# Sums of quarters stored unsplit, steps tied to their groups, and two gate tiles written in source order, in a one-core hybrid trunk kernel

## The chip, the cores and the metric

The kernel runs on one core of a Trainium2 chip. The metric is the device time of one execution in microseconds (us), from runs in which kernels take turns on the same chip. The engines named below are TensorE (PE, with its weight loads PEld), VectorE (DVE), ScalarE (ACT), GpSimd (POOL) and SyncE (SP). SP and POOL issue nearly all DMAs here, each in the order of its own instruction queue.

## The reference, cut to what matters

The program is one layer of a decoder trunk, on 512 prompt tokens and 8 single-token samples, which stand side by side as 520 columns.

```python
def mixer(xn, ...):
    proj = xn @ w_in                       # 2048 x 6160
    bg, cg, hin, q, k, v, og, glr = jnp.split(proj, ...)
    cu, conv_new = causal_dwconv(cg * hin, conv_prev, conv_w)
    ya = bg * cu
    o, s_new = gla_chunked(qh, kh, vh, lf, gla_prev, chunk)
    yb = rms(o) * gla_norm_g * silu(og)
    return concatenate([ya, yb]) @ w_out   # 2048 x 2048

def conv_ffn(xn, prev, w_up, conv_w, conv_b, w_down):
    u, v = jnp.split(xn @ w_up, 2)         # 2048 x 11264
    cu, new = causal_dwconv(u, prev, conv_w)
    return (silu(cu + conv_b) * v) @ w_down, new   # 5632 x 2048

x = x + mixer(rmsnorm(x, norm_mix_g))
x = x + conv_ffn(rmsnorm(x, norm_ffn_g))
y = rmsnorm(x, final_norm_g)
```

## The kernel before

**Numbers.** Every float32 operand of a large product is used as two parts: `hi`, a rounded copy made by ACT, and `lo`, the rest, made by DVE as operand minus `hi` (`split`, L115; `parts`, L101; `prepare`, L1163). A product is three matmuls: hi by hi, hi by the lo of x, lo of the weight by hi. Activations lie transposed, 128 features by 520 columns, as a `hi` and a `lo` tile.

**Stages.** First x is transposed to `xT_d` in DRAM and to the split tiles `xa`. Then come the *plain* groups (`group`, L165): 128 output columns, 16 steps of the contraction, 96 matmuls of 260 columns. For each of the four GLA heads h these are k, q and two of v, and behind each head a tile of the short convolution (`conv_tile`, three groups: cg, hin, bg). The GLA recurrence of a head is a generator in `queue`, of which `tick` takes a step four times a group. At the end of the plain stage stand two tiles of the output gate `og` (L1067). All else of `w_in`, and `w_out`, `w_up` and most of `w_down`, is done with seven products for eight: matrices are seen as 2 by 2 blocks, and `ORDER` lists the seven products, 24 matmuls each. Their weights are raw blocks or sums of blocks, made by DVE (`s<-raw`, L1123) from four loads of 512 KB (`weights`, L1110), and then split. Their activations are seven *forms* of x: forms 1 to 3 are quarters of x themselves, and forms 4 to 7 are sums of quarters. `MIX` lists nine groups of w_in, then follow 8 groups of w_out ("wo"), 44 of w_up ("up") and 20 of w_down ("down").

**Where the sums come from.** For w_in, `mixer_sums(g)` (L665) loads four quarters of x for each g of 0 to 3 from `xT_d`, scales them with the norm's weight on ACT, makes t1, t2, t4 and t3 on DVE and hands each to `stored` (L625): ACT copies hi, DVE subtracts lo, and two DMAs of 260 KB on POOL put them into `mt_d`. That makes 16 sums and 32 stores. `load_mixer_sums(g)` brings back hi and lo of each, 32 loads on POOL. For w_up, `projected(g)` (L1484) does the like behind each of the last four groups of w_out: it stores the new residual (`x1_d`), scales, makes the sums, and `out` (L1510) splits. Form 7, and all forms of the last g, go straight to their place; forms 5, 4 and 6 of g = 0 to 2 go as hi and lo through `t_d`, 18 stores and 18 loads on SP, since their places still hold the inputs of w_out. `load_sum` (L1554) loads them in the last group of w_out.

**What sets the order.** The framework orders the instructions of each engine by its own plan, from priorities (source order) and modelled costs. Where `InOrder` (L57) is called, source order is kept for the engines it names, by dependencies without semaphores. The start of the kernel and the loop over products from L1583 on are kept so; in the loop SP and POOL are kept too. The plain groups, the mixer sums and the two gate tiles are in the planner's order. `extra` (L171) holds the four generators of `mixer_sums`; `group` takes one step of it at its end, from head 1 on, which fixes its place in the source but not in the plan.

**The loop.** For product i, `prepare(i + 2)` splits the weights of two products ahead; `hi` and `lo` have three buffers. `run_steps` calls generators in `steps`, each of which yields the distance from its start, in products, of its next part. Raw weights of the current kind have three buffers (`raw` of pool `weights`), second halves four (pool `raw2`). The SBUF of the GLA pool is used again, after the plain stage, by the pools `yt2`, `raw2` and `sums`; that of `b12` by `yt3`. `yt1`, in place from early on, holds 4 of the 16 places of forms.

Of the kernel before, what the change touches and what calls it, by code (L numbers as in the profile page):

```python
# [37 lines left out]
def trunk_kernel(  # L38
# [18 lines left out]
    class InOrder:  # L57
# [9 lines left out]
        def all(self):  # L67
            return nc.cur_bb.bb.instructions

        def __call__(self):  # L70
# [18 lines left out]
    def two(ap):  # L89
        return ap.rearrange("p (a b) -> p a b", a=2)  # L90
# [565 lines left out]
    def first_tile(kind, g, m):  # L656

        return 4 * g + 2 * m if kind == "down" else 2 * g + 8 * m
# [5 lines left out]

    def mixer_sums(g):  # L665

        def place(n):
            return yt1.tile([P, T], F32, tag=f"y{'hl'[n % 2]}{n // 2 * 4}", name="yx")  # L670

        xg = [place(n) for n in range(4)]
        for q, x in enumerate(xg):
            nc.gpsimd.dma_start(two(x), rows_of(xT_d, "mix", g, q))
        yield
        for q, x in enumerate(xg):
            m = first_tile("mix", g, q // 2)
            for j, h in enumerate(halves(x)):
                nc.scalar.activation(h, h, AF.Copy, scale=gmix[:, m + j : m + j + 1])

        def out(f, t, hi):
            stored(t, [mt_d[f - 4, g, x] for x in range(2)], hi)

        yield
        t1, t2 = xg[0], place(4)
        sub(t1, xg[0], xg[1])
        minus(t2, t1, xg[3])
        out(5, t1, place(5))
        yield
        minus(xg[2], t2, xg[2])  # L690
        out(4, t2, place(6))
        out(7, xg[2], place(7))
        yield
        sub(xg[1], xg[3], xg[1])
        out(6, xg[1], place(5))

    def load_mixer_sums(g):
        for f in (5, 4, 7, 6):
            for x, t in enumerate(form(f, g)):
                nc.gpsimd.dma_start(t.bitcast(F32), mt_d[f - 4, g, x])  # L700

# [31 lines left out]
    with ExitStack() as mix:  # L733
        slots[0::4] = [yt1] * 4
        even, evp = {}, [None]

        def mixed(k):

            if k % 2:
                return tmp()[:, :T]  # L740
            if k < KD // 2:
                even[k] = evp[0].tile([P, T], F32, tag="ye", name="ye")
            else:
                even[k] = zpad[0][:, 2 : 2 + T]
            return even[k]

        def mixed_done(k, y):
            if k % 2 == 0:
                return
            he, dst, i = even.pop(k - 1), g_d[1 - k // 8], k // 2 % 4  # L750
            t21, t34 = pair_sums(he, y)
            for src, f in ((halves(he)[0], 6), (t21, 0), (t34, 2), (y, 4)):
                n = 1 if f == 6 else 2
                stored(src, [dst[f : f + n, x, i] for x in range(2)], tmp())


        def conv_tile(j):
# [10 lines left out]
            ps = group(w_in, j * P, xa)  # L768
            bgr, ya = tmp(), mixed(j)
            evac(ps, bgr[:, :T])  # L770
# [3 lines left out]
        with ExitStack() as gl:  # L774
# [255 lines left out]
            for h in range(NH):  # L1030
                if h == 1:
                    extra.extend(mixer_sums(g) for g in range(4))
                ps = group(w_in, 3584 + h * P, xa) if h else first[0]
# [22 lines left out]
            assert not queue and not extra, (len(queue), len(extra))  # L1056

        yctx = ctx.enter_context(ExitStack())
        yt2 = yctx.enter_context(tc.tile_pool(name="yt2", bufs=1, side="right"))
        slots[1::4] = slots[2::4] = [yt2] * 4  # L1060
        wxr = yctx.enter_context(tc.tile_pool(name="raw2", bufs=4, side="right"))
        wxp = yctx.enter_context(tc.tile_pool(name="sums", bufs=2, side="right"))
        early = second_half(lambda m, k: mix_source(0, m, k))
        for g in range(3):
            load_mixer_sums(g)

        for j in range(2):  # L1067
            og, e, on = tmp(), mixed(8 + j), tmp()
            nc.sync.dma_start(on[:, :T], o_d[j])
            ps = group(w_in, 5120 + j * P, xa)  # L1070
            evac(ps, og[:, :T])
            nc.scalar.activation(e, og[:, :T], AF.Silu)
            nc.vector.tensor_tensor(e, e, on[:, :T], op=ALU.mult)
            mixed_done(8 + j, e)

    bctx.close()
    slots[3::4] = [yctx.enter_context(tc.tile_pool(name="yt3", bufs=1))] * 4
    load_mixer_sums(3)
    for k in range(8):
        for f, kk, b in ((1, k, 0), (2, k + 8, 0), (3, k + 8, 1)):  # L1080
            xq[f, k] = [xa[kk][x][b] for x in range(2)]

# [205 lines left out]
    def mix_gate(n):  # L1288
# [24 lines left out]
        if what == "og":  # L1313
# [10 lines left out]
            mult(v, v, on[1])  # L1324
            yield 4
        dst, i = g_d[1 - k // 8], k // 2 % 4
        t21, t34 = pair_sums(u, v)

        late = n == len(MIX) - 1
        yield 9.5 if late else 4.5  # L1330
# [150 lines left out]

    ssq = []

    def projected(g):  # L1484
# [25 lines left out]
        def out(f, t):  # L1510

            if f == 7 or g == NG - 1:
                split(t, *form(f, g))
            else:
                hi = tmp()[:, :T]
                split(t, hi.bitcast(F32R), t.bitcast(F32R))
                for d, x in zip((t_d[f - 4, g, 0], t_d[f - 4, g, 1]), (hi, t)):
                    nc.sync.dma_start(d, x)

# [33 lines left out]

    def load_sum(f, g):  # L1554
        for x, d in zip(form(f, g), (t_d[f - 4, g, 0], t_d[f - 4, g, 1])):
            nc.sync.dma_start(x.bitcast(F32), d)

# [31 lines left out]
    steps, seeded = [], {}  # L1589
    finish = {"mix": mix_finish, "wo": chunk_finish, "up": up_finish, "down": chunk_finish}  # L1590
    for i, (kind, at, r) in enumerate(order):
# [17 lines left out]
        if j == 0:  # L1609
# [25 lines left out]
        if kind == "wo":  # L1635
# [172 lines left out]
```

## Time and profile before

| what | value |
|---|---|
| time, median of 3 runs | 2238.04 us (2236.33 to 2240.15) |
| the profiled execution's own time | 2237.56 us |
| its span | 2235.9 us, granted TensorE clock 0.987 |
| DVE busy / ACT busy / POOL busy | 78% / 50% / 22% of the span |
| DMA bytes | 430.42 MB, mean 193 GB/s |

The span is the profiled execution from its first to its last instruction; 1.7 us lie around it. A row of the page's groups gives the line, the engine, out<-in, the count, the busy time, the mean of one in ns and the idle time of the engine before them. In a timeline a bracket at the end of a row gives the idle time before it and what ended it. In the view of windows each stretch has its length, the busy time of each engine with the count of instructions, the granted clock, the busy share of the DMA engines (1.0 and a little over is full) and the rate in GB/s.

### The profile page before, as it was taken

What the parts mean: (1) busy time and instruction counts of PE and PEld (TensorE: products, weight loads), DVE (VectorE), ACT (ScalarE), POOL (GpSimd) and SP (SyncE); (2) the same over time, 40 slices, a digit from 0 to 9 for tenths busy, and PEclk for the clock granted to TensorE, in tenths of its full rate; (3) what the DMA queues carried; (4) which work ended last, traced back from release to release, by engine and by line L of the source; (5) the groups of instructions that cost most, each with busy time, mean ns of one, the idle gap of its engine ahead of it and who ended that gap; (6) DMA issues with size and microseconds to landing.
All of it is one profiled execution on the core that took longest, in us unless ns stands there. A gap on an engine that the chain in (4) does not pass through costs nothing.

```text
span 2235.9 us, 43902 instructions
## 1 busy us (share of the span) xinstructions
PE 2167.9 (97%) x17751; PEld 2141.5 (96%) x17751; DVE 1733.5 (78%) x2286; ACT 1114.3 (50%) x1629; POOL 487.5 (22%) x689
## 2 busy tenths in 40 slices
PE   8899999989999998999999999999999999999997
PEld 7889999989999998999999999999999999999997
DVE  5474473638887897888889989899898868888876
ACT  5454353424554475655555555555555554444445
POOL 3353141341223511111311222113121311010000
PEclk9999999999999999999999999999999999999999
DMA  8574444467788999576666766767667868784734
GB/s 249 188 225 123 118 139 120 123 191 211 186 234 262 288 272 300 142 187 172 181 182 165 194 167 182 183 162 194 176 176 198 283 187 224 241 249 142 228 105 152
DMA packets 470103, 430.42 MB, mean 193 GB/s; under 512 B 22489, under 2 KB 423285, under 8 KB 469757
## 3 DMA queue, kind: packets, MB, share of 16 engines
q1 hardware_dynamic: 422001, 289.58, 45.1%
q0 software_dynamic: 46576, 135.82, 22.7%
q8 instruction: 139, 2.28, 0.4%
q10 hardware_dynamic: 1324, 2.23, 0.3%
q14 instruction: 63, 0.52, 0.1%
HBM read 306.91 MB, written 87.76 MB: 177 GB/s over the span
## 4 chain that ended last, share of the span: by engine, by line
PE 83%; DMA 6%; DVE 4%; issue 2%; ACT 2%; SPq 1%; POOL 1%; ACTq 0%; DVEq 0%; POOLq 0%
PE mm L1202 33%; PE ms L1202 14%; PE mm L134 11%; PE x L1442 8%; PE y L1442 8%; PE e L1442 3%; PE f L1442 3%; DMA raw<-in_w_out_dram 1%; DMA yx<-xT_d 1%; PE ms L921 1%; DMA yl<-t_d 1%; DMA raw<-raw 1%; DMA t<-o_d 1%; DVE lo L106 1%; DVE lo L1182 1%
## 5 line engine op out<-in xcount | busy, mean ns | idle before, releaser
L1202 PE MATMUL mm<-yl,hi 128*128 128x260 f32 x1696 | 478.5, 282 | 3.6 <-DVE yl L118 2.8
L1202 PE MATMUL mm<-yh,hi 128*128 128x260 f32 x1696 | 480.0, 283 | 0.8 <-DMA yh<-t_d 0.7
L1202 PE MATMUL mm<-yh,lo 128*128 128x260 f32 x1696 | 478.8, 282 | 0.9 <-DVE lo L1182 0.9
L1178 ACT ACTIVATE hi<-raw 128x1024 fp32r<-128x1024 f32 x324 | 342.4, 1057 | 230.6 <-PE mm L1202 68.5
L1182 DVE TENSOR_TENSOR lo<-raw,hi 128x1024 fp32r<-128x1024 f32 x324 | 395.3, 1220 | 38.1 <-ACT hi L1178 37.6
L1182 DVE TENSOR_TENSOR lo<-s,hi 128x1024 fp32r<-128x1024 f32 x243 | 298.3, 1228 | 129.5 <-ACT hi L1178 124.3
L1178 ACT ACTIVATE hi<-s 128x1024 fp32r<-128x1024 f32 x243 | 257.1, 1058 | 217.0 <-DVE s L1123 79.5
L1202 PEld LDWEIGHTS mm<-yl,hi 128*128 128x128 f32 x1696 | 319.7, 188 | 4.4 <-DVE yl L118 3.0
L1202 PEld LDWEIGHTS mm<-yh,lo 128*128 128x128 f32 x1696 | 319.7, 188 | 1.2 <-DVE lo L1182 1.2
L1202 PEld LDWEIGHTS mm<-yh,hi 128*128 128x128 f32 x1696 | 319.1, 188 | 1.4 <-DMA yh<-t_d 0.7
L1202 PE MATMUL ms<-b,hi 128*128 128x260 f32 x1408 | 258.0, 283 | 0.0
L1202 PEld LDWEIGHTS ms<-b,hi 128*128 128x128 f32 x1408 | 218.1, 189 | 0.0
L1442 PE MATMUL x<-form,hi 128*128 128x260 f32 x1120 | 204.8, 283 | 4.3 <-DVE acc L1461 2.2
L1442 PE MATMUL y<-form,hi 128*128 128x260 f32 x1120 | 204.6, 283 | 2.7 <-DVE acc L1461 2.7
L1123 DVE TENSOR_TENSOR s<-s,raw 128x1024 f32<-128x1024 f32 x162 | 197.9, 1222 | 2.8
L1202 PE MATMUL ms<-b,lo 128*128 128x260 f32 x704 | 199.0, 283 | 0.0
L1442 PEld LDWEIGHTS x<-form,hi 128*128 128x128 f32 x1120 | 172.5, 188 | 5.2 <-issue 2.8
L1442 PEld LDWEIGHTS y<-form,hi 128*128 128x128 f32 x1120 | 172.5, 188 | 3.1 <-ACT hi L1178 3.0
L106 DVE TENSOR_TENSOR lo<-raw,hi 128x1024 fp32r<-128x1024 f32 x76 | 97.2, 1279 | 81.9 <-ACT hi L105 74.4
L1442 PE MATMUL y<-form,lo 128*128 128x260 f32 x560 | 158.4, 283 | 0.0
L1442 PE MATMUL x<-form,lo 128*128 128x260 f32 x560 | 158.3, 283 | 0.0
L1202 PE MATMUL mm<-bh,hi 128*128 128x260 f32 x424 | 121.7, 287 | 15.4 <-DVE t L492 12.6
(359 smaller groups left out, 5164.8 us busy)
## 6 DMA issues: line engine op xcount, KB each, us to landing
raw<-in_w_up_dram SPq DMA_DIRECT2D x176, 512.0 KB
raw<-in_w_down_dram SPq DMA_DIRECT2D x96, 512.0 KB
raw<-in_w_in_dram SPq DMA_DIRECT2D x92, 512.0 KB
form<-f_d SPq DMA_DIRECT2D x126, 260.0 KB
raw<-raw POOLq DMA_DIRECT2D x56, 512.0 KB, 5.9
f_d<-t POOLq DMA_DIRECT2D x80, 260.0 KB, 5.5
raw<-in_w_out_dram SPq DMA_DIRECT2D x32, 512.0 KB
form<-g_d POOLq DMA_DIRECT2D x42, 260.0 KB, 7.6
```

The costliest lines, as they stand in the source:

```text
L106: nc.vector.tensor_tensor(lo, raw, hi.bitcast(F32), op=ALU.subtract)
L134: nc.tensor.matmul(o, w, xx, start=first and i == 0, stop=last and i == 2)
L921: nc.tensor.matmul(pb[:, c * 64 : (c + 1) * 64], L[:, c, :], rhs[:, c], start=True, stop=True,)
L1123: return lambda: nc.vector.tensor_tensor(out, x, y, op=ALU.add)
L1178: nc.scalar.activation(his[i], src, AF.Copy)
L1182: nc.vector.tensor_tensor(los[i], src, his[i].bitcast(F32), op=ALU.subtract)
L1202: nc.tensor.matmul(st["bank"][b], w[:, k, :], x, start=b not in st["used"] and k == 0 and j == 0, stop=k == 7 and j == 2, skip_group_check ...
L1442: nc.tensor.matmul(ps[:, m, :], w[:, k, m * P : (m + 1) * P], x, start=b not in st["used"] and k == 0 and j == 0, stop=k == 3 and j == 2, ...
```

## The change

`mt_d` and `t_d` lose their dimension of hi and lo: a sum goes to DRAM as one float32 tile, and is split after it comes back. `mixer_sums` becomes one generator over g = 1, 2, 3, 0, whose loads are on SP; three of the sums of g = 0 stay in SBUF and are split there, so 13 sums are stored. `group` ties each step of it behind the last instruction that the source has so far on each engine. The two gate tiles move behind the creation of `in_order`, are written out with their loads ahead, and so stand in source order, with the loads of the sums (on SP now), their splits and the start of the first products between them. The second gate's activation and the sums of the two gate tiles (`leave`, formerly the end of `mix_gate`) become steps of the first products. For w_up, nine splits (`split_sums`) follow nine loads at fixed steps of the last group of w_out. `MIX` and the loop are as before.

```diff
+        def after_all(self):
+            self.last = {i.engine: i.name for i in self.all()}
+            return self
...
-        if extra and next(extra[0], extra) is extra:
-            extra.popleft()
+        if extra:
+            step = InOrder(nc.gpsimd.engine, nc.sync.engine).after_all()
+            if next(extra[0], extra) is extra:
+                extra.popleft()
+            step()
...
-    t_d = dp.tile([3, 4, 2, P, T], F32, name="t_d")
-    mt_d = dp.tile([4, 4, 2, P, T], F32, name="mt_d")
+    t_d = dp.tile([3, 3, P, T], F32, name="t_d")
+    mt_d = dp.tile([4, 4, P, T], F32, name="mt_d")
...
+    def mixer_sums():
+        def place(n):
+            return yt1.tile([P, T], F32, tag=f"y{n}", name="yx")
+        for g in (1, 2, 3, 0):
+            xg = [place(n) for n in ("l0 h8 l8 h0" if g % 2 else "l1 l4 h4 h0").split()]
+            for q, x in enumerate(xg):
+                nc.sync.dma_start(two(x), rows_of(xT_d, "mix", g, q))
+            yield
+            for q, x in enumerate(xg):
+                m = first_tile("mix", g, q // 2)
+                for j, h in enumerate(halves(x)):
+                    nc.scalar.activation(h, h, AF.Copy, scale=gmix[:, m + j : m + j + 1])
+                if q == 1:
+                    yield
+            yield
+            t1, t3, t4, b22 = xg
+            t2 = place("h1")
+            sub(t1, t1, t3)
+            minus(t2, t1, b22)
+            yield
+            if g:
+                for f, t in ((5, t1), (4, t2)):
+                    nc.gpsimd.dma_start(mt_d[f - 4, g], t)
+            sub(t3, b22, t3)
+            minus(t4, t2, t4)
+            yield
+            nc.gpsimd.dma_start(mt_d[3, g], t4)
+            if g:
+                nc.gpsimd.dma_start(mt_d[2, g], t3)
+        for f, t in ((5, t1), (6, t3), (4, t2)):
+            split(t, *form(f, 0))
...
+                nc.sync.dma_start(t_d[f - 4, g], t)
...
+    def load_sum(d, f, g):
+        hi, lo = form(f, g)
+        x = lo.bitcast(F32)
+        nc.sync.dma_start(x, d[f - 4, g])
+        return lambda: split(x, hi, lo)
+
+    def split_sums():
+        for n in (4, 4.5, 5.5, 6, 6.5, 7.5, 8.5, 9, 9.5):
+            yield n
+            loaded.popleft()()
...
     in_order = InOrder(nc.gpsimd.engine, nc.sync.engine)
-    mult(R2, R, R)
...
+    raws = [load_og(n) for n in range(3)]
+    ws = [parts(*raws[0])]
+    raws.append(load_og(3))
+    early = second_half(lambda m, k: mix_source(0, m, k))
+    on = [tmp()[:, :T] for _ in range(2)]
+    for j, x in enumerate(on):
+        nc.sync.dma_start(x, o_d[j])
+    put = [load_sum(mt_d, f, g) for f in (5, 4) for g in range(1, 4)]
+    ws.append(parts(*raws[1]))
+    ps = new_mm()
+    span(ps, ws[0], xa, 0, 0, 8, KD)
+    ws.append(parts(*raws[2]))
+    span(ps, ws[1], xa, 8, 8, 8, KD)
+    ws.append(parts(*raws[3]))
     begin(0)
     load_rest(0)
+    put += [load_sum(mt_d, 6, g) for g in range(1, 4)]
+    y8, y9 = zpad[0][:, 2 : 2 + T], tmp()[:, :T]
+    evac(ps, y8)
+    nc.scalar.activation(y8, y8, AF.Silu)
+    mult(y8, y8, on[0])
+    ps = new_mm()
+    span(ps, ws[2], xa, 0, 0, 8, KD)
     prepare(0)
+    for x in put[:3]:
+        x()
+    span(ps, ws[3], xa, 8, 8, 8, KD)
     prepare(1)
+    for x in put[3:6]:
+        x()
+    evac(ps, y9)
+    mult(R2, R, R)
...
+    put += [load_sum(mt_d, 7, g) for g in range(4)]
...
+    def second_gate():
+        yield 0.5
+        nc.scalar.activation(y9, y9, AF.Silu)
+        yield 1
+        mult(y9, y9, on[1])
+        yield 4
+        yield from leave(8, y8, y9)
+
+    def put_sums():
+        for x, n in zip(put[6:], (1, 1.5, 2, 3.5, 4, 4.5, 5)):
+            yield n
+            x()
...
+                if at[1] == NG - 1:
+                    steps.append([split_sums(), i, 0])
...
-                    load_sum(f, h)
+                    loaded.append(load_sum(t_d, f, h))
```

More of the change, by code (lines that the diff above doesn't have):

```diff
@@ L663, in rows_of @@
         return d[m : m + 2, :, b * HT : (b + 1) * HT].rearrange("m p c -> p m c")
-    def mixer_sums(g):
+    def mixer_sums():
         def place(n):
[L670 to L700, printed above, removed]
+            return yt1.tile([P, T], F32, tag=f"y{n}", name="yx")
[25 more added lines that the diff above has]
+                nc.gpsimd.dma_start(mt_d[2, g], t3)
@@ L733, in trunk_kernel @@
     with ExitStack() as mix:
-        slots[0::4] = [yt1] * 4
+        for n in (0, 1, 4, 8):
+            slots[n] = yt1
         even, evp = {}, [None]
[L737 to L745, printed above, removed]
         def mixed_done(k, y):
@@ L749, in mixed_done @@
                 return
-            he, dst, i = even.pop(k - 1), g_d[1 - k // 8], k // 2 % 4
+            he, dst, i = even.pop(k - 1), g_d[1], k // 2
             t21, t34 = pair_sums(he, y)
@@ L768, in conv_tile @@
             ps = group(w_in, j * P, xa)
-            bgr, ya = tmp(), mixed(j)
+            bgr, ya = tmp(), tmp()[:, :T]
+            if j % 2 == 0:
+                even[j] = ya = evp[0].tile([P, T], F32, tag="ye", name="ye")
             evac(ps, bgr[:, :T])
@@ L1031, in trunk_kernel @@
                 if h == 1:
-                    extra.extend(mixer_sums(g) for g in range(4))
+                    extra.append(mixer_sums())
                 ps = group(w_in, 3584 + h * P, xa) if h else first[0]
@@ L1056, in trunk_kernel @@
             assert not queue and not extra, (len(queue), len(extra))
[L1058 to L1081, printed above, removed]
     for dst, src in ((new_conv_s, state_conv), (new_ffn_s, state_ffn_conv)):
@@ L1325, in mix_gate, with leave @@
             yield 4
+        yield from leave(k, u, v, n == len(MIX) - 1)
+    def leave(k, u, v, late=False):
         dst, i = g_d[1 - k // 8], k // 2 % 4
         t21, t34 = pair_sums(u, v)
-        late = n == len(MIX) - 1
         yield 9.5 if late else 4.5
@@ L1479, in chunk_finish @@
             onto(2, "a", ALU.subtract)
-    ssq = []
+    ssq, loaded = [], deque()
     def projected(g):
@@ L1514, in out @@
             else:
[L1515 to L1518, printed above, removed]
+                nc.sync.dma_start(t_d[f - 4, g], t)
         yield 4.5
@@ L1583, in trunk_kernel, with load_og @@
     in_order = InOrder(nc.gpsimd.engine, nc.sync.engine)
-    mult(R2, R, R)
+    yctx = ctx.enter_context(ExitStack())
+    yt2 = yctx.enter_context(tc.tile_pool(name="yt2", bufs=1, side="right"))
+    for n in (2, 3, 5, 6, 7, 9, 10, 11):
+        slots[n] = yt2
+    wxr = yctx.enter_context(tc.tile_pool(name="raw2", bufs=4, side="right"))
+    wxp = yctx.enter_context(tc.tile_pool(name="sums", bufs=2, side="right"))
+    og = [(5120 + j * P, k0) for j in range(2) for k0 in (0, 8)]
+    def load_og(n):
+        c0, k0 = og[n]
+        return load(w_in, k0, 8, c0, P)
+    raws = [load_og(n) for n in range(3)]
[12 more added lines that the diff above has]
+    ws.append(parts(*raws[3]))
     begin(0)
     load_rest(0)
+    put += [load_sum(mt_d, 6, g) for g in range(1, 4)]
[5 more added lines that the diff above has]
+    span(ps, ws[2], xa, 0, 0, 8, KD)
     prepare(0)
+    for x in put[:3]:
+        x()
+    span(ps, ws[3], xa, 8, 8, 8, KD)
     prepare(1)
-    steps, seeded = [], {}
+    for x in put[3:6]:
+        x()
+    evac(ps, y9)
+    mult(R2, R, R)
+    bctx.close()
+    yt3 = yctx.enter_context(tc.tile_pool(name="yt3", bufs=1))
+    slots[12:] = [yt3] * 4
+    put += [load_sum(mt_d, 7, g) for g in range(4)]
+    for k in range(8):
+        for f, kk, b in ((1, k, 0), (2, k + 8, 0), (3, k + 8, 1)):
+            xq[f, k] = [xa[kk][x][b] for x in range(2)]
+    def second_gate():
[9 more added lines that the diff above has]
+            x()
+    steps, seeded = [[second_gate(), 0, 0], [put_sums(), 0, 0]], {}
     finish = {"mix": mix_finish, "wo": chunk_finish, "up": up_finish, "down": chunk_finish}
```

3 lines of the change are left out of this document (removed).

## The prediction

> **What bounds the kernel now.** I read the page's busy shares first, then the view of windows, then the timelines of the three stretches in which PE falls short.
>
> ```profile
> PE 2167.9 (97%) x17751; PEld 2141.5 (96%) x17751; DVE 1733.5 (78%) x2286; ACT 1114.3 (50%) x1629; POOL 487.5 (22%) x689
> ...
> 70.00:170.00 100.00, 88.83 (x684) 84.86 (x683) 58.48 (x95) 50.24 (x91) 47.13 (x75) 0.93 0.73 231
> 200.00:300.00 100.00, 96.68 (x764) 92.43 (x764) 51.54 (x87) 42.29 (x64) 30.08 (x33) 0.98 0.37 108
> 300.00:400.00 100.00, 99.69 (x812) 96.44 (x811) 52.27 (x88) 40.59 (x62) 28.28 (x33) 1.00 0.47 132
> 480.00:530.00 50.00, 35.66 (x277) 34.77 (x277) 23.65 (x31) 14.79 (x20) 19.82 (x34) 0.86 1.00 291
> 530.00:630.00 100.00, 100.00 (x837) 100.00 (x836) 85.62 (x111) 50.55 (x72) 16.40 (x23) 1.00 0.74 189
> 785.00:863.00 78.00, 71.50 (x585) 70.37 (x584) 77.14 (x95) 61.12 (x99) 13.55 (x16) 1.00 0.99 275
> 863.00:890.00 27.00, 22.35 (x136) 20.99 (x137) 14.60 (x19) 12.87 (x21) 2.03 (x3) 0.81 1.10 310
> ```
>
> PE is the bound, and only stretches in which it issues less can give time. Columns are stretch, length, busy PE, PEld, DVE, ACT, POOL (with counts), clock, DMA share, GB/s. The row 530 to 630 is PE at full rate: 837 matmuls in 100 us, 8.37 a us, so 24 matmuls (one product) take 2.87 us and a group of seven 20.1 us. By that yardstick a stretch loses its length less count / 8.37. Head 0 of the GLA, with all of the mixer sums in it (70 to 170): 100 - 81.7 = **18.3 us**. Head 1, which has none (200 to 300): 8.7; further heads (300 to 400): 3.0. The passage from plain groups to products (480 to 530): 50 - 33.1 = **16.9 us**. The passage from w_out to w_up: 78 - 69.9 = 8.1 and 27 - 16.2 = 10.8, together **18.9 us**. The change touches these three and little else.
>
> **Part A: steps of the mixer sums tied to their groups.** The planner has drawn them all into head 0.
>
> ```profile
> 70.00:170.00 100.00, 23.45 (x32) 24.31 (x48) 28.64 (x48) 0.93 0.73 231
> 200.00:300.00 100.00, 0.00 (x0) 0.00 (x0) 0.00 (x0) 0.98 0.37 108
> 93.93 0.92 ACT L679 ACTIVATE yx<-yx,par 128x260 f32<-128x260 f32 x2 [7.16 <-DMA yx<-xT_d]
> 96.03 0.51 ACT L679 ACTIVATE yx<-yx,par 128x260 f32<-128x260 f32 x1 [1.19 <-issue]
> 96.45 1.04 ACT L105 ACTIVATE hi<-raw 128x1024 fp32r<-128x1024 f32 x1
> 97.53 1.23 DVE L106 TENSOR_TENSOR lo<-raw,hi 128x1024 fp32r<-128x1024 f32 x1 [9.98 <-ACT hi L105]
> PE ms L798 <- DVE v L492: 7.0, 3, 6.0
> ```
>
> The first two rows are the windows of the tile `yx` alone (DVE, ACT, POOL): 23.45 + 24.31 us in 100 on DVE and ACT, none later. The next four are the harm: ACT stands 7.16 and 1.19 us before a scaling that waits for its quarter of x, and the weights' `hi` and `lo` behind it come 9.98 us late. PE waits 6.0 us once for an evacuation on DVE in the same place.
>
> Tied steps come one per group, and head 1's first group takes the first. A group is 96 / 8.37 = 11.5 us, while a transfer of such a tile lands in 4.8, at most 6.9:
>
> ```profile
> DMA to landing us min/median/max: 2.3/4.8/6.9
> ```
>
> So the scaling should find its data, and the sums, a step later, need no wait; POOL's store comes a step behind the sum. The loads move to SP, behind the group's weights; they add 16 issues there, and 32 stores on POOL become 13. Without the steps head 0 should lose what head 1 loses: 18.3 - 8.7 = 9.6. I take off 1.6 for steps that now lie in heads 1 to 3, whose DVE and ACT are busy about half of the time: **gain 8**. Ends: -3, if a scaling still stands in front of the weights, and now in four heads; 12, if head 0 falls nearer to the 3.0 of the later heads.
>
> **Part B: the two gate tiles and the passage to the products.**
>
> ```profile
> 490.00:500.00 10.00, 2.71 (x23) 2.50 (x21) 0.00 (x0) 0.00 (x0) 5.48 (x11) 0.81 1.05 372
> 503.61 1.22 DVE L1123 TENSOR_TENSOR s<-raw 128x1024 f32<-128x1024 f32 x1 [23.75 <-issue]
> 504.76 0.76 DVE L492 TENSOR_TENSOR t<-mm,R 128x260 f32<-128x260 f32 x2
> PE mm L1202 <- DVE t L492: 12.6, 1, 12.6
> 475.72 3.92 DMA g_d<-ye
> 479.76 1.61 SPq L720 DMA_DIRECT2D raw<-in_w_in_dram  x2
> 481.46 9.57 SPq L1119 DMA_DIRECT2D raw<-in_w_in_dram  x1
> 480.64 0.55 POOL L700 DMA_DIRECT2D yh<-mt_d  x1
> ...
> 503.05 0.54 POOL L700 DMA_DIRECT2D yl<-mt_d  x1
> 476.28 4.36 POOL L633 DMA_DIRECT2D g_d<-t  x6
> yh<-mt_d POOLq DMA_DIRECT2D x12, 260.0 KB, 6.2
> ```
>
> PE ends the second gate tile at about 492.7 (2.71 us busy from 490) and stands until 505.3, because the evacuations of both gate tiles (L492) are queued on DVE behind the first sum of weights (L1123), which stands 23.75 us for loads issued at 479.76. Meanwhile POOL issues 24 loads of `mt_d`, 6.4 MB, and the DMA engines are full.
>
> New order on DVE: the first gate tile's evacuation stands ahead of that sum, so PE has PSUM. What is late next is the weights. The loads at 479.76 start when the store of `ye` from the GLA pool lands (475.72 + 3.92), and that stays. Behind them SP now issues, in order, two loads of `o_d`, six unsplit sums, then the raw block of product 0: 1024 + 520 + 1560 + 512 KB = 3.7 MB. About 1.6 MB of the `g_d` stores of 476 to 480 run beside it. At 330 GB/s, between the 291 and 372 of the rows, 5.3 MB take 16 us: landing at 496, plus hi 1.06 and lo 1.22 (rows of L1178 and L1182 below): product 0 at 498.5, a gap of **5.8 instead of 12.6**. Ends: 489.6 (3.7 MB alone at 372, no gap) and 498 (5.3 MB at 291, product 0 at 500.3).
>
> ```profile
> L1178 ACT ACTIVATE hi<-raw 128x1024 fp32r<-128x1024 f32 x324 | 342.4, 1057 | 230.6 <-PE mm L1202 68.5
> L1182 DVE TENSOR_TENSOR lo<-raw,hi 128x1024 fp32r<-128x1024 f32 x324 | 395.3, 1220 | 38.1 <-ACT hi L1178 37.6
> 476.81 1.91 DVE L118 TENSOR_TENSOR t<-t 128x520 fp32r<-128x520 f32 x3
> ```
>
> Then DVE bounds. From hi 0 (497.1), at the 1.13 that such operations stand apart: lo 0 1.1; six splits of sums at 1.91 / 3 = 0.64, 3.8; lo 1 and a sum 2.3; the second evacuation and R2 1.4: 505.7. Then lo 2 to 7 and three sums of weights 10.2, seven more splits 4.5, the second gate's multiply 0.7, its pair sums and first split 2.1: product 7 at about **523**. Before, of the 277 matmuls from 480 to 530 some 84 (ten us at full rate) and 23 belong to the gate tiles; 170, 7.1 products, came from 505 to 530, so product 7 stood near 529. **Gain 6**; ends -2 (a tile of the ring of eight `tmp` that a load of `o_d` needs is released only by the last `g_d` store, and SP's list stands behind it) and 11.5 (no gap).
>
> [...]
>
> **Part C: the sums for w_up.**
>
> ```profile
> 807.00:829.00 22.00, 20.71 (x171) 20.37 (x170) 21.90 (x28) 17.46 (x28) 4.24 (x6) 1.00 0.98 264
> t_d<-t SPq DMA_DIRECT2D x18, 260.0 KB
> 862.95 10.40 DMA yl<-t_d
> 876.31 0.70 DVE L118 TENSOR_TENSOR b<-t,b 128x520 fp32r<-128x520 f32 x1 [6.17 <-DMA x_d<-acc]
> PE mm L1202 <- DVE yl L118: 2.8, 1, 2.8
> PE mm L1202 <- DVE acc L1461: 2.8, 1, 2.8
> ```
>
> Here DVE is the bound: 21.90 of 22 us, and a group takes 22 instead of 20.1. Nine splits (0.61 apart) leave the stretch to 863, of which five come back in the last group (steps 4 to 6.5) and four after it: 4 x 0.61 = 2.4 us earlier at the first product of w_up. Nine stores and nine loads of 260 KB go, 4.8 MB; at 275 to 310 GB/s that is 16 us of DMA time in the 92 us or so in which the engines are full. So the waits for `x_d<-acc` (6.17) and behind it 2.8 of PE, and a part of the slow clock at 0.81, should shrink: of the 10.8 lost after 863 I take 4. Against it stands a new wait: split (5,0) follows its load by about 2.5 products, 7 us, and a load took up to 10.40; behind the split on ACT and DVE stand the next `hi` and `lo`, for which PE has two products, 5.7 us, in hand. I take 1.4 for it. **Gain 5**; ends -6 and +12.
>
> The slow clock I leave in the sums: 0.81 after the 2.8 us waits shows that gaps smaller than mine cost it too. [...]
>
> **The sum.** 8 + 6 + 5 = 19. The profiled execution took 2237.56 us (span 2235.9 and 1.7 around it): 2218.6. It stands 0.5 under the median of the runs, 2238.04, so for the median **2219**.
>
> **The rivals.**
>
> *Transfers get out of the way altogether.* SP's loads land by 489.6 and the steps cost heads 1 to 3 nothing: A 9.6, B 11.5, C 10, 31 in all: 2207. For it speaks that 13 sums are read in the first passage instead of 24, 2.9 MB less; against it that DVE has 13 splits more to do between products, and that SP's list starts no earlier than 479.6.
>
> *The waits only change names.* The planner, which ties nothing forward, still puts a scaling still puts a scaling in front of weights (A 0), the loads of `o_d` wait for the last `g_d` store (476.28 + 4.36 + 10.1, the row below, = 490.7) so that, with 2.3 MB to follow at 291 (7.9) and 2.3 for hi and lo, product 0 stands at 501 and product 7 at 525.5 (B 3), and the splits of C wait (C 1): 2238 - 4 = 2234. That is also what the change gives if it does not do what it says.
>
> ```profile
> DMA to landing us min/median/max: 2.2/6.4/10.1
> ```
>
> *Slower: the nine splits stand in front of the weights.* In C a split that waits for its load holds ACT and DVE, in order, and through them all `hi` and `lo`. If each load is as late as the worst of before, 10.4 against the 7.2 it is given, nine times 3.2 is 29 us; less the 5.7 in hand, 23 lost, against A and B: 2238 - 14 + 23 = 2247. It decides from (14 + 5.7) / 9 = 2.2 us a split. Against it: the loads come in pairs and land together, and the DMA engines have 4.8 MB less.
>
> **How the numbers follow.** About 0.2%, 4.5 us, is what a measurement of this kernel can tell from no change. Forecast near 2219 (2210 to 2229): 0.5. Out of the way (2200 to 2210): 0.2. Names only (2229 to 2242): 0.22, of which 0.14 are within 0.2% and 0.08 under it. Slower: 0.08. Faster is 0.5 + 0.2 + 0.08 = 0.78, same 0.14, slower 0.08. The range leaves out the slower case, and of the others some 0.06 at each end: 2204 to 2236. It holds each part's ends taken singly (A -3 to 12 alone moves the sum from 2230 to 2215, B -2 to 11.5 from 2227 to 2213.5, C -6 to 12 from 2230 to 2212).
>
> **What would show it.** A: no ACT idle before L679 at 90 to 100, its 32 scalings spread from about 100 to 400, and 70 to 170 with some 760 matmuls. B: L492 of the first gate ahead of L1123, PE idle of 3 to 8 us, then DVE over 90% busy for 25 us. C: w_up's first product 2 to 4 us earlier against its own group, DMA share under 1.0 from 800 to 860. Wrong would be: ACT standing for `yx` in heads 1 to 3; product 0 waiting on a load beyond 503; `lo` of w_up's weights standing behind splits that wait for `t_d`.

## The result, and the profile after

| kernel | median us (range, runs) | ratio to before, 95% interval |
|---|---|---|
| before | 2239.10 (2236.33 to 2242.33, 4 runs) | 1 |
| after | 2217.68 (2216.27 to 2225.22, 4 runs) | 0.9911 [0.9884, 0.9937] |
| after once more (e1) | 2219.36 (2217.29 to 2223.34, 4 runs) | 0.9914 [0.9894, 0.9933] |

Each ratio, here and below, is to the runs of before that were taken in turn with it; their medians lie from 2239.03 to 2240.09. The change is faster by 20 to 21 us; 2219 was forecast. The profiled execution of after, 2225.22 us, is the longest of its four, so its rows overstate the time by some 7 us; where a stretch of it differs from that in other executions of the same program, the text says so. Lines have moved: the plain group's matmul is now L139, the products' L1177, a split L122 and L123, the products' hi and lo L1153 and L1157, the evacuation L500, the sums of weights L1098.

The page of after, its busy line, then its view of windows, in the columns known from before:

```profile
PE 2165.0 (97%) x17751; PEld 2140.5 (96%) x17751; DVE 1734.3 (78%) x2286; ACT 1113.7 (50%) x1629; POOL 447.2 (20%) x622
```

```profile
70.00:170.00 100.00, 98.82 (x814) 95.94 (x813) 44.64 (x76) 35.91 (x59) 18.09 (x27) 1.00 0.45 128
200.00:300.00 100.00, 94.23 (x734) 90.49 (x733) 52.06 (x85) 45.88 (x78) 27.97 (x34) 0.95 0.44 130
300.00:400.00 100.00, 98.15 (x782) 94.46 (x782) 54.13 (x91) 40.89 (x65) 32.49 (x39) 0.98 0.50 148
500.00:510.00 10.00, 7.94 (x62) 7.30 (x61) 10.00 (x15) 6.14 (x10) 0.00 (x0) 1.00 0.65 167
510.00:520.00 10.00, 8.94 (x73) 8.54 (x72) 9.92 (x16) 5.84 (x10) 1.10 (x2) 1.00 0.65 174
530.00:630.00 100.00, 100.00 (x836) 100.00 (x836) 87.79 (x114) 52.10 (x75) 20.75 (x29) 1.00 0.78 204
817.00:839.00 22.00, 22.00 (x185) 21.94 (x184) 21.90 (x27) 16.38 (x26) 5.13 (x6) 1.00 1.08 272
839.00:853.00 14.00, 8.11 (x56) 7.94 (x55) 9.47 (x13) 8.23 (x14) 1.75 (x2) 0.76 1.05 315
```

The busy times of PE, DVE and ACT are those of before within 3 us; only POOL's fell, by 40.3. What changed is where PE stands idle. Head 0 (70 to 170) holds 814 matmuls instead of 684: by the yardstick of 8.37 a us that is 15.5 us. The stretches 200 to 300 and 300 to 400 give back 3.6 each (734 instead of 764, 782 instead of 812). From 500 to 520 DVE is busy without a break. From 839 to 853 stands a hole that is new.

The waits of PE in after, over the whole run (engine, line, what it waited for, us in total, times, longest):

```profile
PE mm L139 <- ACT hi L110: 10.2, 2, 7.9
PE y L1420 <- DVE acc L1439: 5.9, 1, 5.9
```

The 12.6 us before product 0 are gone, and so is one of the two waits of 2.8 at w_up, that for `yl`; the other, for `acc`, is still there with 3.1 (2.2 in e1). Two waits take their place: 7.9 us ahead of the first gate tile and 5.9 in the last group of w_out. Both are in the second execution as well (7.76 and 6.12), so they belong to the program.

To see where the 20 us come from, the run is cut at points that every trace has: the end of PE's first wait for k of head 0 (near 70 us), the end of the last plain group ahead of the gate tiles, and the first matmul of the products, of w_out, of w_up and of w_down. Each stretch is the difference of two such times in PE's timeline.

| stretch, us | before | after | e1 |
|---|---|---|---|
| heads: k to the end of the last convolution group | 399.8 | 390.5 | 389.5 |
| from there to product 0 | 35.8 | 32.9 | 34.0 |
| product 0 to w_out | 188.0 | 189.3 | 187.1 |
| w_out to w_up | 170.0 | 172.8 | 174.2 |
| w_up to w_down | 897.7 | 890.9 | 889.9 |

For before, the end of the last group is product 0's start less the 12.6 us and the 23.2 of two gate tiles (192 matmuls, with their ends). The stretches of after are shorter by 14.9 us together and those of e1 by 16.6, and both start some 2 us later than those of before, so the two columns do not hold all of the 20 to 21 us: both profiled executions are the longest of their four. Where the others save the rest, no trace shows.

### The profile page after: what moved, and what is told of

It is laid out like the page before. It is cut to its first block, busy times and chain, and to the rows that moved or that the text cites. A ratio compares the mean times of both kernels' runs of the same rounds, so it can differ in the third digit from the quotient of the medians.

```text
span 2223.5 us, 43796 instructions
## 1 busy us (share of the span) xinstructions
PE 2165.0 (97%) x17751; PEld 2140.5 (96%) x17751; DVE 1734.3 (78%) x2286; ACT 1113.7 (50%) x1629; POOL 447.2 (20%) x622
## 4 chain that ended last, share of the span: by engine, by line
PE 77%; DVE 2%; DMA 2%; issue 1%; SPq 1%; ACT 1%; POOL 0%; ACTq 0%; DVEq 0%
PE mm L1177 34%; PE ms L1177 13%; PE x L1420 9%; PE y L1420 9%; PE mm L139 5%; PE e L1420 3%; PE f L1420 3%; DMA raw<-in_w_down_dram 1%; DVE lo L1157 1%; DVE yl L123 0%; DMA yl<-mt_d 0%; DMA yl<-t_d 0%; SPq L727 0%; PE ms L1758 0%; PE ms L921 0%
## 5 line engine op out<-in xcount | busy, mean ns | idle before, releaser
L1177 PE MATMUL mm<-yh,hi 128*128 128x260 f32 x1696 | 480.0, 283 | 2.2 <-ACT ms L1187 1.4
L1177 PE MATMUL mm<-yh,lo 128*128 128x260 f32 x1696 | 478.2, 282 | 0.6 <-DVE lo L1157 0.6
L1177 PE MATMUL mm<-yl,hi 128*128 128x260 f32 x1696 | 478.4, 282 | 0.1
L1153 ACT ACTIVATE hi<-raw 128x1024 fp32r<-128x1024 f32 x324 | 342.6, 1057 | 232.4 <-PE mm L1177 68.9
L1157 DVE TENSOR_TENSOR lo<-raw,hi 128x1024 fp32r<-128x1024 f32 x324 | 395.8, 1222 | 41.9 <-ACT hi L1153 41.3
L1157 DVE TENSOR_TENSOR lo<-s,hi 128x1024 fp32r<-128x1024 f32 x243 | 298.5, 1228 | 127.3 <-ACT hi L1153 122.2
L1153 ACT ACTIVATE hi<-s 128x1024 fp32r<-128x1024 f32 x243 | 256.9, 1057 | 217.4 <-DVE s L1098 81.1
L1177 PEld LDWEIGHTS mm<-yh,hi 128*128 128x128 f32 x1696 | 318.7, 188 | 2.6 <-ACT ms L1187 1.6
L1177 PEld LDWEIGHTS mm<-yh,lo 128*128 128x128 f32 x1696 | 319.3, 188 | 1.0 <-DVE lo L1157 1.0
L1177 PEld LDWEIGHTS mm<-yl,hi 128*128 128x128 f32 x1696 | 319.1, 188 | 0.3 <-DVE yl L123 0.3
L1177 PE MATMUL ms<-b,hi 128*128 128x260 f32 x1408 | 255.8, 281 | 0.0
L1177 PEld LDWEIGHTS ms<-b,hi 128*128 128x128 f32 x1408 | 216.8, 188 | 0.0
L1098 DVE TENSOR_TENSOR s<-s,raw 128x1024 f32<-128x1024 f32 x162 | 198.0, 1222 | 2.8
L1177 PE MATMUL ms<-b,lo 128*128 128x260 f32 x704 | 198.7, 282 | 0.0
L110 ACT ACTIVATE hi<-raw 128x1024 fp32r<-128x1024 f32 x76 | 79.7, 1052 | 115.2 <-PE mm L139 93.8
```

The costliest lines, as they stand in the source:

```text
L110: nc.scalar.activation(hi, raw, AF.Copy)
L1098: return lambda: nc.vector.tensor_tensor(out, x, y, op=ALU.add)
L1153: nc.scalar.activation(his[i], src, AF.Copy)
L1157: nc.vector.tensor_tensor(los[i], src, his[i].bitcast(F32), op=ALU.subtract)
L1177: nc.tensor.matmul(st["bank"][b], w[:, k, :], x, start=b not in st["used"] and k == 0 and j == 0, stop=k == 7 and j == 2, skip_group_check ...
```

## The experiments

Unless another kernel is named, an edit is made in after.

### The changed kernel again

> The changed kernel as it is, to see an execution nearer to its median, since the profiled one took 2225.22 us and the other three 2216 to 2218. If the two new waits of that profile (7.9 us of PE before the first gate tile, 5.9 us before the last products of w_out, where ACT stood 6.6 for a load of t_d) belong to the program, they are here too, and the 7 us lie elsewhere. If they are chance, they are gone or far smaller here, at 2217 in all.

Measured 2219.36, above. The two new waits are not chance.

### Part A: the tie, and the sums that became lighter

The tie alone, put into the kernel before:

```diff
+        def after_all(self):
+            self.last = {i.engine: i.name for i in self.all()}
+            return self
...
-        if extra and next(extra[0], extra) is extra:
-            extra.popleft()
+        if extra:
+            step = InOrder(nc.gpsimd.engine, nc.sync.engine).after_all()
+            if next(extra[0], extra) is extra:
+                extra.popleft()
+            step()
```

> The kernel before with one part of the change: the steps of the mixer sums tied behind their groups (sums still stored split, on POOL; the gate tiles and w_up as before). Theory, order: the scaling no longer stands in front of the weights' hi in head 0, the window 70 to 170 goes from 684 matmuls to about 760, and the time falls by 7 to 9, from 2239 to about 2231. Rival, bytes: the gain of the change comes from fewer DMA bytes, which are all here; 2238 to 2240.

Measured 2246.64 us, ratio 1.003 [1.0019, 1.0041]: slower than before. The windows of e2, and then its waits:

```profile
70.00:170.00 100.00, 98.51 (x804) 95.31 (x805) 45.39 (x78) 36.99 (x60) 21.85 (x33) 1.00 0.48 139
300.00:400.00 100.00, 91.89 (x700) 87.94 (x699) 46.51 (x80) 40.57 (x66) 30.12 (x40) 0.93 0.53 155
400.00:460.00 60.00, 54.85 (x423) 51.70 (x423) 36.96 (x58) 18.37 (x31) 23.26 (x33) 0.94 0.53 155
```

```profile
  POOL mt_d L640: 67.4, 15
  ACT yx L686: 14.5, 5
```

(These two rows list who waited for the tile `yx`, in us and times.) Head 0 is nearly as quick as in after (804 matmuls). But the loss has moved to the later heads: 700 matmuls from 300 to 400, where before had 812. POOL's stores, tied in order, wait 67.4 us for their sums, and in this kernel the loads of the next quarters stand behind them on POOL; so ACT then waits 14.5 us for quarters, five times. To test that, the loads alone were put on SP:

```diff
-            nc.gpsimd.dma_start(two(x), rows_of(xT_d, "mix", g, q))
+            nc.sync.dma_start(two(x), rows_of(xT_d, "mix", g, q))
```

> The kernel before with the tie alone, as e2 (2246.6), and the loads of the quarters of x on SP instead of POOL. Theory: in e2 the loads stood on POOL behind stores that wait for their sums, so that a late sum held up the next one's loads; with the loads on SP the stretches 300 to 400 and 400 to 460 come back from 700 and 423 matmuls to 780 to 812 and 485 to 492, and the time is 2226 to 2236. Rival: it is the work of the steps themselves (splits, two stores each) in the later heads that costs: 700 to 740 matmuls there again, 2243 to 2248.

Measured 2236.11, ratio 0.9991 [0.9981, 1.0]. The windows of e12, and who waited for `yx` there:

```profile
300.00:400.00 100.00, 96.71 (x778) 93.18 (x778) 58.66 (x98) 44.76 (x72) 34.80 (x48) 1.00 0.59 172
400.00:460.00 60.00, 55.22 (x425) 52.13 (x424) 24.76 (x40) 19.46 (x29) 13.58 (x17) 0.94 0.45 130
```

```profile
  POOL mt_d L640: 60.0, 15
...
  ACT yx L686: 5.0, 1
```

POOL's stores still wait, 60.0 us, but nothing that ACT needs stands behind them: ACT's wait for quarters falls from 14.5 to 5.0, the stretch from 300 comes back to 778 matmuls, and some 10 us return. So with the tie, the queue of the loads decides whether it costs or not. The rival has a part too: 400 to 460 does not come back (425 against the 485 forecast), and the whole is only 3 us better than before, with an interval that reaches no change. The stretches of the table say where: the heads take 399.8 us in before, 409.8 in e2 and 394.8 in e12, but from there to product 0 e12 loses 3.0 of its 5.0 again (38.8 against 35.8). The opposite experiment takes the tie out of after and leaves the lighter sums:

```diff
         if extra:
-            step = InOrder(nc.gpsimd.engine, nc.sync.engine).after_all()
             if next(extra[0], extra) is extra:
                 extra.popleft()
-            step()
```

> The changed kernel with the tie alone taken out of the group. Theory, order: the planner draws the steps into head 0 again, whose 100 us from 70 lose some 18 again, and the time rises by 6 to 9, to about 2225. Rival, bytes: steps with a single float32 store are light enough wherever they stand; 2217 to 2219.

Measured 2222.36, ratio 0.9928 [0.9905, 0.9951]. Its windows:

```profile
70.00:170.00 100.00, 94.89 (x762) 91.39 (x761) 53.30 (x90) 45.82 (x81) 23.68 (x38) 0.98 0.60 179
300.00:400.00 100.00, 100.00 (x816) 96.99 (x816) 52.24 (x86) 40.26 (x62) 29.10 (x33) 1.00 0.48 132
```

Without the tie the planner draws the scalings forward again (76 to 108 us), yet product 0 starts at 494.8, as in after (495.0), and the heads take 389.1, within the 386.0 to 390.5 of the kernels with the tie. Most of part A is therefore what e3 keeps: three splits in the heads instead of 16, 13 stores instead of 32, loads on SP. With the tie in, the loads on SP are worth 15.0 us of the heads (e2 to e12) and the fewer splits and stores 4 to 9 (e12 to after); without it the three were not taken apart. The tie itself moves the loss about: against e3, after has 52 matmuls more in head 0, and 31 and 34 fewer from 200 to 300 (734 against 765) and from 300 to 400. What it adds by the medians, 3 to 5 us, lies within overlapping intervals.

### Part B: what sets product 0

In after the hole stands ahead of the gate tiles. SP's, ACT's and PE's timelines of after; a bracket is the idle time before the row and its cause:

```profile
463.16 0.99 SPq L1027 DMA_DIRECT2D o_d<-o  x2
464.20 7.38 SPq L100 DMA_DIRECT2D raw<-in_w_in_dram  x4
...
487.17 0.38 SPq L1094 DMA_DIRECT2D raw<-in_w_in_dram  x1
```

```profile
466.32 1.78 ACT L122 ACTIVATE t<-t 128x520 fp32r<-128x520 f32 x3 [7.10 <-DVE t L594]
468.86 1.06 ACT L110 ACTIVATE hi<-raw 128x1024 fp32r<-128x1024 f32 x1 [0.76 <-DMA raw<-in_w_in_dram]
...
493.77 1.06 ACT L1153 ACTIVATE hi<-raw 128x1024 fp32r<-128x1024 f32 x1 [7.15 <-DMA raw<-in_w_in_dram]
```

```profile
469.97 0.58 PE L139 MATMUL mm<-bh,hi 128*128 128x260 f32 x1 [7.87 <-ACT hi L110]
```

In source order on SP the loads of the gate tiles' weights (464.20) stand behind the stores of the last head's o (463.16), which wait for that head's end. In before the planner had issued them ahead:

```profile
443.84 8.80 SPq L95 DMA_DIRECT2D raw<-in_w_in_dram  x2
...
470.88 1.01 SPq L1027 DMA_DIRECT2D o_d<-o  x2
```

e4 clears SP by putting those two stores on POOL:

```diff
-                    nc.sync.dma_start(o_d[2 * h + d], o[:, d, :])
+                    (nc.gpsimd if h == NH - 1 else nc.sync).dma_start(o_d[2 * h + d], o[:, d, :])
```

> The changed kernel with the last GLA head's two stores of o_d issued by POOL instead of SP. Theory: PE's 7.9 us before the first gate tile come from SP's queue, in which all four weight loads of the gate tiles stand behind these stores (issued at 463.2, the loads from 464.2 on); the loads then go when buffers are free, 445 to 460, that wait is gone, and a part of it, 2 to 5 us, comes back before product 0, whose loads still start when the GLA pool is released: 2210 to 2215. Rival: the loads wait for their buffers or for the pool, not for the queue; nothing moves, 2217 to 2219.

Measured 2213.48, ratio 0.9888 [0.9871, 0.9904]. ACT's timeline of e4:

```profile
459.46 1.78 ACT L122 ACTIVATE t<-t 128x520 fp32r<-128x520 f32 x3 [7.09 <-DVE t L594]
461.14 2.94 ACT L110 ACTIVATE hi<-raw 128x1024 fp32r<-128x1024 f32 x3
```

The four blocks of gate weights are now loaded from 438.73 on, and the wait of PE is still 7.00. It has only changed its owner: hi stands on ACT, in source order, behind the splits of the last convolution pair, which wait for DVE. The rows of after had both causes: there the same splits hold ACT until 468.1, and the load adds only 0.76. From the last group to product 0 it takes 31.8 us instead of 32.9 (after) or 34.0 (e1). That is 1 to 2 of the 4 to 6 us by which the median is lower; the heads take 386.3, but they take 386.0 to 386.8 in e5, e6 and e8 too, which leave those stores as they are in after. Where the rest comes from, no run shows. e7 adds to e4 that three of the four loads for the gate tiles, and the splits of the first two, are stated behind the last convolution group:

```diff
...
+            if j == NH - 1:
+                raws.extend(load_og(n) for n in range(3))
+                ws.extend(parts(*raws[n]) for n in range(2))
...
-    raws = [load_og(n) for n in range(3)]
-    ws = [parts(*raws[0])]
     raws.append(load_og(3))
...
-    ws.append(parts(*raws[1]))
```

> The run with the stores of o_d on POOL, and in addition the first three weight loads and the first two splits of the gate tiles stated in the source behind the last group of the convolution, ahead of its evacuation. Theory: what holds the gate tiles after the loads are freed is the order on ACT and DVE, where their hi and lo stand behind the splits of the last convolution pair (hi at 461.1 behind L122 at 459.5); stated earlier they run under that group, the 7.0 us of PE are gone, and 2 to 5 us of it return before product 0, whose raw block lands later than PE is ready; 2208 to 2211. Rival: the convolution's end on DVE and POOL, not the order, sets it (the bank of PSUM or the GLA's end); the wait stays near 7 and the time at 2213.

Measured 2213.46, ratio 0.9882 [0.9859, 0.9905]: the hole ahead of the gate tiles is gone, and the time is that of e4. ACT's timeline of e7 says why:

```profile
466.34 1.04 ACT L110 ACTIVATE hi<-raw 128x1024 fp32r<-128x1024 f32 x1
...
487.29 1.06 ACT L1163 ACTIVATE hi<-raw 128x1024 fp32r<-128x1024 f32 x1 [15.48 <-DMA raw<-in_w_in_dram]
```

PE now stands 6.4 us in front of product 0, whose raw block SP issues at 479.77, behind the second halves, two tiles of o and six sums; the second halves are what holds the list, since SP stands 18.0 us there for the store of `ye`, until 467.24. This is a gap at the place of the 5.8 that the prediction had: it was covered by the other hole. e9 joins e7 to a later order of the splits for w_up (e5, below), and e10 also puts that one block at the head of the list, ahead of the second halves (against e9):

```diff
-            None if n else early,
+            None,
...
-    early = second_half(lambda m, k: mix_source(0, m, k))
+    begin(0)
...
-    begin(0)
     load_rest(0)
```

> The edits of e7 (last head's stores of o on POOL, gate tiles' weights stated behind the last convolution group) and of e5 (splits of the sums for w_up from 5.5 on) in one kernel. If their gains lie in different stretches, the first product comes at 488 to 490 as in e7 and the stretch from the first w_out product to the first w_up product is 169 to 170 us as in e5 instead of 172.8: 2210 to 2212. If both only move a loss into the same later stretch, 2213 to 2215.

> As e9, and the raw block of product 0 is loaded ahead of the second halves, the outputs of the GLA and the six mixer sums on SP (begin(0) in place of the second halves' loads, which then follow in their usual place). Theory: what holds product 0 in e7 (6.4 us of PE idle on the ACT rounding of its block) is the block's place in SP's list, so the wait falls to 0 to 3 us, the first product comes at 483 to 486, and the time is 2205 to 2209. Rival: ACT and DVE are full there and product 0 only swaps this wait for one on the forms of product 1 or on the evacuations: first w_out product not earlier than in e9, 2210 to 2213.

Measured: e9 2214.93 (2211.79 to 2217.4), ratio 0.9889 [0.9875, 0.9904]; e10 **2207.34** (2206.92 to 2208.66), ratio **0.9857 [0.9843, 0.9872]**, the fastest of all, 32 us under before. SP's and ACT's timelines of e10:

```profile
461.57 0.37 SPq L1104 DMA_DIRECT2D raw<-in_w_in_dram  x1
468.08 1.10 SPq L727 DMA_DIRECT2D raw<-in_w_in_dram  x2
469.22 3.67 SPq L1591 DMA_DIRECT2D t<-o_d  x2
472.94 5.51 SPq L1543 DMA_DIRECT2D yl<-mt_d  x6
```

```profile
471.31 1.04 ACT L1163 ACTIVATE hi<-raw 128x1024 fp32r<-128x1024 f32 x1
480.16 0.64 ACT L122 ACTIVATE yh<-yl 128x520 fp32r<-128x520 f32 x1 [7.81 <-DMA yl<-mt_d]
```

The block is issued at 461.57 instead of 480.77 (e9), its hi needs no wait at 471.31, and the first product starts at 481.4 instead of 490.0. Counted from the last convolution group, product 0 comes 7.9 us earlier (22.9 against 30.8). The whole of that reaches the first w_out product (670.0 instead of 679.3) and the end (the median is 7.6 lower): the theory holds, and the rival, that DVE or ACT would take it back, does not. The block's place in SP's list had set product 0. e9 by itself adds nothing to e7: 490.0 at product 0, and what it gains from w_out to w_up (170.3) it has lost by w_down (891.0 against 888.4 in e7). The test of bytes issues each load of a sum twice:

```diff
         nc.sync.dma_start(x, d[f - 4, g])
+        if d is mt_d:
+            nc.sync.dma_start(x, d[f - 4, g])
```

> The changed kernel with each load of a mixer sum from DRAM issued twice (13 loads of 260 KB more, 3.4 MB). It asks what bytes cost in the passage from plain groups to products, where the DMA share is 0.65 to 1.0. Theory: the transfers set the landing of product 0's block and of the later sums, so the six more loads ahead of that block (1.56 MB, 4 to 6 us at 256 to 344 GB/s) put the first product 4 to 6 us later than 495: 2222 to 2225. Rival: the order on SP and ACT sets it and bytes do not: first product 495 to 496, 2217 to 2220.

Measured 2244.58, ratio 1.0026 [1.0014, 1.0037], far past both forecasts. SP's timeline of e11:

```profile
478.94 0.42 SPq L1533 DMA_DIRECT2D yl<-mt_d  x1
484.18 0.32 SPq L1535 DMA_DIRECT2D yl<-mt_d  x1
484.55 0.42 SPq L1533 DMA_DIRECT2D yl<-mt_d  x1
487.56 0.32 SPq L1535 DMA_DIRECT2D yl<-mt_d  x1
...
501.86 0.43 SPq L1094 DMA_DIRECT2D raw<-in_w_in_dram  x1
```

The second load writes the tile of the first, so in e11 SP waited until the first had landed: the two issues of a pair stand 5.2 us apart, and then 3.0. It is thus no measurement of bytes, and what 1.6 MB cost there stays open. But it shows the same chain from the other side: the block is issued 14.7 us later than in after (501.86 against 487.17), product 0 comes 12.2 later (507.2; 16.7 later when counted from the last group), and the seven further pairs cost 11 more by w_out (200.2 from product 0, against 189.3).

That DVE bounds the first products was tested by leaving out seven of its subtractions there:

```diff
-        return lambda: split(x, hi, lo)
+        def put(last=True):
+            nc.scalar.activation(hi, x, AF.Copy)
+            if last:
+                nc.vector.tensor_tensor(lo, x, hi.bitcast(F32), op=ALU.subtract)
+
+        return put
...
-            x()
+            x(False)
```

> The changed kernel with the subtraction of lo left out in the seven sums that are split between the first products (ACT's hi stays; lo keeps the unsplit sum). Theory: DVE bounds the first seven products, and 7 x 0.61 = 4.3 us of it go: from product 0 to the first product of w_out 2 to 4 us less than the 187 to 189 of the changed kernel, and 2215 to 2217 in all. Rival: the weights' loads bound them; within 1 us.

Measured 2217.62, ratio 0.9909 [0.9885, 0.9934]. One stretch in the windows of e8, and then the same stretch of after:

```profile
500.00:530.00 30.00, 30.00 (x252) 30.00 (x251) 27.41 (x37) 19.43 (x31) 6.33 (x9) 1.00 0.78 203
```

```profile
500.00:530.00 30.00, 26.87 (x216) 25.85 (x215) 29.85 (x41) 18.66 (x31) 4.91 (x7) 1.00 0.70 182
```

With DVE relieved PE has no gap (30.00 of 30), where after has 26.87. But product 0 starts at 491.0 in e8 and 495.0 in after, so the two windows do not hold the same work. From 9 to 39 us behind product 0, PE is busy for 30.00 us in e8 and for 28.3 to 29.6 in after, e1, e4, e5 and e6, which are one program there. So DVE does bound PE in that stretch, at 0.4 to 1.7 us. Little of it is left behind it: product 7 starts 22.8 us behind product 0 in e8, and 22.9 (e6) to 26.1 (after) in the others; product 0 to w_out takes 186.0 in e8 and in e6, and the median shows nothing.

### Part C: the sums for w_up

The timelines of SP, ACT and DVE in after, around the new hole:

```profile
836.06 2.17 SPq L1533 DMA_DIRECT2D yl<-t_d  x2
```

```profile
844.19 0.64 ACT L122 ACTIVATE yh<-yl 128x520 fp32r<-128x520 f32 x1 [6.62 <-DMA yl<-t_d]
844.73 1.04 ACT L1153 ACTIVATE hi<-raw 128x1024 fp32r<-128x1024 f32 x1
```

```profile
844.86 0.70 DVE L123 TENSOR_TENSOR yl<-yl,yh 128x520 fp32r<-128x520 f32 x1 [3.34 <-ACT yh L122]
...
848.51 0.69 DVE L1439 TENSOR_TENSOR acc<-acc,y 128x520 f32<-128x520 f32 x1
```

ACT stands 6.62 us for split (5,0), whose load was issued 8.1 us before, and the next weights' hi stands behind it. So ACT had come to the split 1.5 us after the load's issue. DVE stands 3.34 us for it in turn, and the accumulation that PE waits for, at 848.51, comes behind that. e6 undoes part C alone (hi and lo through DRAM, as before):

```diff
...
-                nc.sync.dma_start(t_d[f - 4, g], t)
+                hi = tmp()[:, :T]
+                split(t, hi.bitcast(F32R), t.bitcast(F32R))
+                for d, x in zip((t_d[f - 4, g, 0], t_d[f - 4, g, 1]), (hi, t)):
+                    nc.sync.dma_start(d, x)
...
```

> The changed kernel with the sums for w_up stored and loaded as hi and lo again (18 stores, 18 loads, no splits behind the loads). Theory: of part C, w_out itself is 4 us shorter this way (170 us from its first product to the first of w_up instead of 174), and the first products of w_up 8 us longer; the net is 3 to 5 us slower, about 2223. Rival: the later start alone moves that stretch, and part C is worth nothing; 2219.

Measured 2220.39, ratio 0.9917 [0.9898, 0.9936], which by itself can't be told from after. The stretches can: w_out to w_up 170.3, w_up to w_down 897.3, together 1067.6, as in before (1067.7); in after, e1, e3, e4 and e8, which have part C and its splits as written, the sum is 1063.1 to 1064.7. So part C is worth 3 to 4.6 us against before: 7 to 8 gained behind the first w_up product, 2.5 to 4 lost ahead of it. e5 moves the first splits back:

```diff
-        for n in (4, 4.5, 5.5, 6, 6.5, 7.5, 8.5, 9, 9.5):
+        for n in (5.5, 5.5, 6, 6.5, 6.5, 7.5, 8.5, 9, 9.5):
```

> The changed kernel with the first five splits of the sums for w_up later: steps 5.5, 5.5, 6, 6.5, 6.5 of the last group of w_out instead of 4, 4.5, 5.5, 6, 6.5. Theory: PE's 5.9 to 6.1 us before the last products of w_out come from ACT, which stands 6.6 us at the first split for a load of t_d, ahead of the next hi; a product and a half later that load has landed, the wait goes to under 2, and the time falls by 3 to 5, from 2219 to about 2215. Rival: DVE bounds the stretch in any case, and five splits pressed into a shorter stretch stand in front of the last sums of w_out; the time stays within 1 us.

Measured 2214.36, ratio 0.9889 [0.987, 0.9908]. The timeline of PE in e5:

```profile
848.25 0.56 PE L1177 MATMUL mm<-bh,hi 128*128 128x260 f32 x1 [7.32 <-DVE acc L1439]
```

No split up to the first w_up product waits over 1.5 us for its load any more, and w_out to w_up falls to 169.6 (170.3 and 170.4 in e9 and e10). But PE then stands 7.32 for the last accumulations of w_out, where after had 5.9 and 3.1. Both stretches together take 1059.5, 1061.3 and 1061.2 in the three kernels, against 1063.1 to 1064.7 above; but e7, with the early splits, has 1061.1. So the later splits are worth 0 to 5 us. e5's median is lower by 3 to 5, but its product 0 already came at 490.3, ahead of any edited line.

## Why the prediction was right

The sum held: 19 forecast, 20 to 21 measured. That it came so near is in part luck, since A gave more than its term and B less. The terms, with e1, e4, e5, e6 and e8 beside after wherever their program is that of after in the stretch (e4 but for two stores at the end of the heads):

| part | forecast | measured | from |
|---|---|---|---|
| A | 8 (-3 to 12) | 9 to 14 | heads 386.0 to 390.5 against 399.8 |
| B | 6 (-2 to 11.5) | 2 to 3 to product 0, then -1 to 2 | 32.9 to 34.1 against 35.8; 186.0 to 189.3 against 188.0 |
| C | 5 (-6 to 12) | 3 to 4.6 | 1063.1 to 1064.7 against 1067.7 |

**A, right in kind, too small.** "Without the steps head 0 should lose what head 1 loses" was too careful: with 814 matmuls head 0 loses 2.7, not the 8.7 of head 1. "I take off 1.6 for steps that now lie in heads 1 to 3" was too little: those stretches gave back 3.6 each. Named as cause was the tie. e2, e3 and e12 show that it isn't the main one: alone it gains 3 us at best and loses 7 with the loads on POOL, and the lighter sums keep most of the gain without it. The sentence "The loads move to SP" was counted only as 16 issues; beside the tie it is worth 15.0 us of the heads. The scalings are spread as forecast, from 113 to 368 us. One sign of being wrong did show: ACT stands 5.5 us for `yx` at 350 in after, and 5.5 in e1. Of the rows read for before, the 1.19 us ahead of a scaling are marked "issue", not a quarter of x; nothing in the sum hangs on them.

**B, the gap right, its place wrong.** The step that failed is "The loads at 479.76 start when the store of `ye` from the GLA pool lands, and that stays": it weighed SP's list from 479.6 on, and not what source order does ahead of it, to the gate tiles' own loads and hi. There the 7.9 us arose, and behind it the gap of 5.8 could not be seen; e7 opened it again, at 6.4. That the list ahead of the raw block sets product 0 was right, as e10 and e11 show from both sides; but the wait for `ye` is that of the second halves, not of the block, which e10 issues 6.5 us ahead of them, and by it B was worth some 8 us more than the change took. Counted to product 7, as the forecast did, from the end of the last convolution group, B gave some 2 (after) to 4 us (e6), not 6. That DVE bounds the first products was right, for 0.4 to 1.7 us.

**C, right in the net, by two errors that cancel.** "I take 1.4 for it" stands against a wait of PE of 5.7 to 6.1 (after, e1, e4, e8). The load was not late, with 8.1 us from its issue to the split where up to 10.40 was reckoned with; what failed is that the split "follows its load by about 2.5 products, 7 us": ACT came to it 1.5 us after the issue. So "2.4 us earlier at the first product of w_up" became 2.5 to 4 later. In return 7 to 8 us came back behind that product, not 4. "DMA share under 1.0" did not come true: it is 1.08 from 817 to 839. The rival of the late splits decided from 2.2 us a split on; in after it was one split that PE waited for, not nine. That the next weights' hi and lo stood behind it is the sign of being wrong that was named for C.

**What stays open.** Kernels that are the same program in the heads differ by some 4 us there (386.0 to 390.5), and by as much in the time at which the heads begin (68.9 to 72.8), and no run shows why. What the tie adds on top of the lighter sums, and what the bytes of the sums cost, were not settled.

## What to carry to other kernels

Where work is put into source order, look first at what then stands *behind* a waiting instruction on each queue: loads behind stores that wait cost 10 us here, and one raw block moved to the head of SP's list gained some 8. A wait that vanishes when its cause is taken away and returns one place further (7.9, 7.0, 6.4) is one chain: take the next link, too, before judging the first. When terms of a sum are to be told apart, compare stretches between fixed points of the program, which told the 3 to 4.6 us of part C from nothing where medians did not.

## What the runs showed of the hardware

In e11 each load into a tile that another load was still filling stood on SP until the first had landed, and everything behind it stood too: 13 waits of SP, 38.1 us together, for 260 KB each. The granted clock in or behind the new holes was 0.63 from 470 to 475 in after, behind the 7.9 us, 0.76 from 839 to 853 there, with the wait of 5.9 in it, and 0.81 from 490 to 500 in e9, where PE had stood 7.7 us. In before it was 0.81 from 863 to 890, where the longest wait of PE was 2.8 us, and 0.50 from 879 to 882.
